# A two-layer decoder kernel: two more gate/up groups as seven products, with weight sums made earlier

## The chip, the cores and the metric

The kernel runs on one core of one Trainium2 chip. The metric is the device time of one execution in microseconds; lower is better. One execution was also recorded by the hardware profiler. In this text PE is TensorE (matmuls), DVE is VectorE, ACT is ScalarE, POOL is GpSimd and SP is the engine whose queue issues the DMA transfers. Each engine works through its own instruction queue in order; they meet by semaphores.

## The reference

Two decoder layers over 1024 tokens of width 1024, float32 throughout:

```python
for l in range(DEPTH):                       # 2
    h = rmsnorm(x, attn_norm[l])
    proj = h @ w_in[l]                       # one projection for four token mixers
    ...                                      # latent attention, gated convolution,
                                             # causal pooling, sliding-window attention
    x = x + mixed @ w_o[l]
    h2 = rmsnorm(x, ffn_norm[l])
    gate, up = jnp.split(h2 @ w_gate_up[l], 2, axis=-1)   # 1024 x 5632
    x = x + (jax.nn.silu(gate) * up) @ w_down[l]
return rmsnorm(x, final_norm)
```

The change concerns `h2 @ w_gate_up[l]` and what goes on around it.

## The kernel before

**Products.** A float32 product is made of three fp32r matmuls: both operands are split into a rounded high part and a low rest, and high·high, high·low and low·high are added in PSUM (`mm3`, L255). ACT makes the high part (a cast, L280, or a scaled copy with the norm's gain, L285) and DVE the low part (a subtraction, L283 or L286). A product of a 512 by 128 weight block with 512 by 512 activations is four such triples: 12 matmuls of 128x512.

**Gate/up in groups.** The 5632 columns of `w_gate_up` are worked in 22 groups `f`, each with 128 gate and 128 up columns. The 1024 inputs are taken as two halves and the 1024 tokens as two halves, so that a group is a 2 by 2 block product: eight products of 12 matmuls. From group 3 on a group is made by seven products (a Winograd form of Strassen's scheme), named after the activation operand: B11, B21, N2, N1, T3, B22, T4. They need four combined weight blocks and four combined activation blocks. B11, B21, B12 and B22 are the plain activation halves.

- `combine(j)` (L1117) makes the combined activations N1, N2, T3, T4 of block `j` (four blocks): two scaled copies on ACT, four operations on DVE, and four splits into high and low parts.
- `GateUp` (L1182) loads a group's two weight halves (two DMAs of 512 KB). `sums` (L1191) has POOL make three weight sums, `sum4` (L1215) the fourth; `split1` to `split4` split the weights and sums into high and low parts. `split_plain` splits the two raw halves only.
- Groups 0, 1 and 2 are plain: `plain(f, u)` (L1331) issues the four products of one token half `u`. `plain_gates` and `plain_acts` evacuate them: a multiplication with the row scale `r2` from the RMS norm, the silu on ACT, a scaling on POOL (L1370), and the product with the up half on DVE.

**Around it.** `out_last` (L1148) makes the last of the output projection, one token half at a time: eight outputs `d`, each an addition on DVE, a split with gain, a store to DRAM and a sum of squares for the norm. `ss2.rnorm` turns the sums into the row scale: a matmul against ones and three ACT operations (L349 to L351), two of which need a table other than the silu's. `combine` needs the outputs of both token halves. After it come groups 3 to 21 in a loop, whose weight sums are made two groups ahead.

**Memory.** `F` and `R` are pools of 128x512 float32 slots in SBUF for raw and split data (`half` takes one, `pair` two). A slot is waited for until its last reader is done. PSUM has eight banks of 128x512.

**What sets the order.** The program is traced in the order in which it is written and then planned: `Order` (L1715) estimates when each instruction could run on each engine (SP with eight transfers in flight), ranks them by what follows from them, picks the best of a few passes, assigns PSUM banks from the planned times, and imposes the order on each engine's queue. `need` (L1733 on) lists what each instruction has to wait for; `users` (L1747) adds waits for a slot's earlier users to the later users of a buffer.

Of the kernel before, what the change touches and what calls it, by code (L numbers as in the profile page):

```python
# [51 lines left out]
class Slots:  # L52
# [59 lines left out]
def trunk_kernel(ctx: ExitStack, tc: tile.TileContext, ins, out, given=None):  # L112
# [165 lines left out]
    def split(hi, lo, f, gain=None, after=None):  # L278
        if gain is None:
            a = act.copy(hi, f)  # L280
            if after is not None:
                behind(a, after)
            dve.tensor_tensor(out=lo, in0=f, in1=rd(hi), op=ALU.subtract)  # L283
        else:
            a = act.activation(hi, f, AF.Copy, scale=gain)  # L285
            dve.scalar_tensor_tensor(  # L286
                out=lo, in0=f, scalar=gain, in1=rd(hi), op0=ALU.mult, op1=ALU.subtract
            )
# [129 lines left out]
    for l in range(L):  # L418
# [698 lines left out]
        def combine(j):  # L1117

            (a0, b0), (a1, b1) = [[F.ap(x[2 * j + n][t]) for t in HALVES] for n in range(2)]
            c = PC_FFN + 2 * j  # L1120
            g0, g1, n = pcol(l, c), pcol(l, c + 1), l * NK + 2 * j + 1
            v0, v1 = tmp("te"), tmp("te")
            act.activation(v0, b0, AF.Copy, scale=g0)
            act.activation(v1, b1, AF.Copy, scale=g1)
            n1, n2, t3, t4 = tmp("tp"), tmp("tp"), tmp("tp"), tmp("tp")
            dve.scalar_tensor_tensor(
                out=n1, in0=a0, scalar=g0, in1=v0, op0=ALU.mult, op1=ALU.subtract
            )
# [13 lines left out]
            hb[T4][j] = half_split(t4)  # L1142
            for n in range(2):
                for u in range(2):
                    F.free(x[2 * j + n][u])
# [22 lines left out]
                for s in hl:  # L1168
                    R.free(s)

        def gu_load(f):
            raw = F.pair(), F.pair()
            for n in range(2):
                sp.dma_start(F.ap2(raw[n]), ins["w_gu"][l, f, n])
            return raw

        def pair_split(s, after=None):
            h, lo = R.pair(), R.pair()
            split(R.ap2(h), R.ap2(lo), F.ap2(s), after=after)
            return h, lo  # L1180

        class GateUp:  # L1182

            def __init__(self, f):
                self.raw = F.pair(), F.pair()
                for n in range(2):
# [14 lines left out]

            def split1(self):
                self.s1 = pair_split(self.raw[0])

            def split2(self):
                F.free_pair(self.raw[0])
                self.s2 = pair_split(self.raw[1])

            def split3(self):
                self.sq = pair_split(self.q)
                F.free_pair(self.q)

# [2 lines left out]
                pool.tensor_tensor(out=q4, in0=q4, in1=F.ap(self.raw[1] + 1), op=ALU.add)  # L1217

            def split4(self):
                self.s4 = half_split(F.ap(self.raw[1]))  # L1220
                F.free_pair(self.raw[1])

        def product(p, w, b, start=True, stop=True, again=False):
            terms = []
# [101 lines left out]
        std[1].split_plain()  # L1326


        acts = {f: [None, None] for f in range(3)}

        def plain(f, u):  # L1331

            w, b = std[f], ((B11, B21), (B12, B22))[u]
# [5 lines left out]
            waiting.append((f, u, pg, pu))  # L1339
            if u != (f == 2):  # L1340
                for i in w.s1 + w.s2:
                    R.free_pair(i)

# [3 lines left out]
        def plain_gates():  # L1347
            for f, u, pg, pu in waiting:
                gate = tmp("tp")
                mul_to(gate, pg, r2[u])  # L1350
                silu(gate, r2[u])
                gates.append((f, u, gate, pu))
            waiting.clear()

        def plain_acts():
            for f, u, gate, pu in gates:
                acts[f][u] = F.half()
                mul_to(F.ap(acts[f][u]), pu, gate)
            gates.clear()
# [139 lines left out]
        plain(0, 1)  # L1499
        std[2].split_plain()  # L1500
        combine(2)
        plain(1, 1)
        w = GateUp(3)
        plain_gates()
        w.sums()
        w.split1()
        combine(3)
        plain_acts()
        plain(2, 1)
# [6 lines left out]
        plain_acts()  # L1516
        wn = GateUp(4)
        plain(2, 0)
        w.sum4()
        w.split4()  # L1520
        wn.sums()
        plain_gates()
        plain_acts()
        sp.dma_start(ad_of(B11, 0), F.ap(acts[0][HALVES.index(0)]))
        combos(0)
        for f in range(3, NFF):
# [188 lines left out]
class Order:  # L1715
# [9 lines left out]
    def __init__(self, traced, edges, banks=True):  # L1725
        self.n = len(traced)
        self.engine = [self.queue(i) for i in traced]
        self.cost = [self.costs(i) for i in traced]
        self.kind = [self.kinds(i) for i in traced]
        self.moved = [self.passing(i) for i in traced]  # L1730
        place = {i.name: k for k, i in enumerate(traced)}
        need = [{} for _ in traced]
        users = self.users = defaultdict(list)  # L1733
        for k, i in enumerate(traced):
            for m in {a.memref for a in (*i.outs, *i.ins) if hasattr(a, "memref")}:
                users[m].append(k)
# [373 lines left out]
```

## Time and profile before

| | |
|---|---|
| median of 3 runs | 2056.87 us (2054.34 to 2056.95) |
| profiled execution, its own time | 2056.29 us |
| its span, first to last instruction | 2054.5 us |
| mean granted TensorE clock | 0.998 |
| PE, DVE, ACT, POOL busy | 2039.0, 1509.7, 984.6, 526.5 us |
| DMA traffic | 290.81 MB, mean 142 GB/s |

The page of the profile shows one execution. Its first part gives each engine's busy time, its share of the span and its instructions. The second part cuts the span into 40 equal slices and gives the busy share of each in tenths. The fourth follows the chain of work that ended last back from the last instruction. Groups of instructions read: line, engine, operation, outputs from inputs, shapes, count, then busy time and mean duration in ns, then the idle time before them with what ended it. A timeline row reads: start, duration, engine, line, operation, operands, count and, in brackets, the idle time of the engine before it and who ended that. Two rows of DVE overlap a little: the next starts before the last has drained, so back-to-back work is counted from start to start.

### The profile page before, as it was taken

How to read it: one execution, taken by the hardware profiler on the slowest of the kernel's cores; microseconds unless marked ns; L12 is line 12 of the kernel's file. 1: busy time of each engine (PE TensorE's matmuls, PEld its weight loads, DVE VectorE, ACT ScalarE, POOL GpSimd, SP SyncE). 2: the span in 40 equal slices, each digit the busy share in tenths (PEclk: the TensorE clock that was granted, in tenths of full speed). 3: DMA queues.
4: the chain of work that ended last, by engine and by line, in shares of the span. 5: the costliest groups of instructions: out<-in, count | busy, mean ns of one | idle time of the engine just before them, and what ended most of it. 6: DMA issues, size and time to landing. Idle time of an engine off the chain costs nothing.

```text
span 2054.5 us, 26467 instructions
## 1 busy us (share of the span) xinstructions
PE 2039.0 (99%) x9470; PEld 1685.7 (82%) x9470; DVE 1509.7 (73%) x2423; ACT 984.6 (48%) x1723; POOL 526.5 (26%) x404
## 2 busy tenths in 40 slices
PE   9999999999999999999999999999999999999998
PEld 7887888888888888888888878877888888888887
DVE  8779978976677668555657898889766766775555
ACT  7447746843333335444533666667333333354342
POOL 0000000046776772000000000000567767710000
PEclk9999999999999999999999999999999999999999
DMA  5101222425555547766401112133355555487642
GB/s 182 45 32 46 86 77 75 159 108 172 182 168 189 179 166 258 248 211 214 145 31 44 37 44 96 60 111 124 112 183 182 172 186 176 151 302 235 205 170 96
DMA packets 138083, 290.81 MB, mean 142 GB/s; under 512 B 13408, under 2 KB 60512, under 8 KB 137952
## 3 DMA queue, kind: packets, MB, share of 16 engines
q1 hardware_dynamic: 137952, 289.13, 41.2%
q8 instruction: 74, 1.21, 0.2%
q14 instruction: 57, 0.47, 0.1%
HBM read 204.66 MB, written 83.36 MB: 140 GB/s over the span
## 4 chain that ended last, share of the span: by engine, by line
PE 94%; DVE 3%; DMA 1%; ACT 1%; issue 1%; SPq 0%; DVEq 0%; POOL 0%; ACTq 0%
PE ps_mm L260 36%; PE ps_s L260 28%; PE ps_t L260 12%; PE ps_pv L260 8%; PE ps_pv L1025 2%; PE ps_t L1013 1%; PE ps_s L959 1%; PE ps_s L960 1%; PE ps_s L961 1%; PE ps_pv L634 1%; DMA u<-in_w_gu 1%; PE ps_s L573 1%; PE ps_s L831 1%; PE ps_t L622 1%; PE ps_t L343 1%
## 5 line engine op out<-in xcount | busy, mean ns | idle before, releaser
L260 PE MATMUL ps_mm<-u,u 128*128 128x512 f32 (+1 forms) x3376 | 829.1, 390 | 1.3 <-DVE u L1064 1.0
L260 PEld LDWEIGHTS ps_mm<-u,u 128*128 128x128 f32 x3376 | 614.7, 188 | 126.8 <-issue 4.6
L260 PE MATMUL ps_s<-u,u 128*128 128x512 f32 x2676 | 634.2, 389 | 1.3 <-DVE u L359 0.4
L260 PEld LDWEIGHTS ps_s<-u,u 128*128 128x128 f32 x2676 | 501.8, 188 | 108.5 <-DVE u L283 1.0
L283 DVE TENSOR_TENSOR u<-u,u 128x1024 fp32r<-128x1024 f32 (+2 forms) x392 | 457.8, 1184 | 158.9 <-ACT u L280 97.0
L280 ACT CAST u<-u 128x1024 fp32r<-128x1024 f32 (+2 forms) x392 | 339.1, 883 | 486.5 <-PE ps_mm L260 186.3
L260 PE MATMUL ps_t<-u,u 128*128 128x512 f32 (+1 forms) x1212 | 274.1, 378 | 0.3 <-DVE u L1363 0.3
L260 PEld LDWEIGHTS ps_t<-u,u 128*128 128x128 f32 x1212 | 219.0, 188 | 43.1 <-DVE u L1363 0.7
L1370 POOL TENSOR_TENSOR tp<-tp,u 128x512 f32<-128x512 f32 x88 | 145.3, 1651 | 348.9 <-ACT tp L1369 348.9
L1022 POOL MEMSET u<- 128x128 f32 x32 | 5.4, 205 | 880.6 <-PE ps_mm L260 418.2
L260 PE MATMUL ps_pv<-u,u 128*128 128x512 f32 x696 | 164.9, 389 | 0.0
L260 PEld LDWEIGHTS ps_pv<-u,u 128*128 128x128 f32 x696 | 130.6, 188 | 27.1
L1369 ACT ACTIVATE tp<-tp 128x512 f32<-128x512 f32 x88 | 55.6, 632 | 153.9 <-DVE tp L359 153.8
L280 ACT CAST u<-ps_t 128x512 fp32r<-128x512 f32 (+3 forms) x132 | 65.3, 503 | 51.3 <-PE ps_t L1013 25.9
L1448 POOL TENSOR_TENSOR u<-u 128x352 f32<-128x352 f32 x64 | 79.3, 1239 | 38.9 <-DMA u<-in_w_dn 34.0
L1217 POOL TENSOR_TENSOR u<-u 128x512 f32<-128x512 f32 x38 | 78.4, 2063 | 23.3 <-DVE u L283 22.1
L285 ACT ACTIVATE u<-u,par 128x512 fp32r<-128x512 f32 x100 | 69.9, 716 | 25.4 <-DVE u L359 7.9
L283 DVE TENSOR_TENSOR u<-ps_t,u 128x512 fp32r<-128x512 f32 (+3 forms) x132 | 75.5, 581 | 7.4 <-ACT u L280 6.5
L286 DVE SCALAR_TENSOR_TENSOR u<-u,par,u 128x512 fp32r<-128x512 f32 x100 | 73.2, 746 | 6.5 <-ACT u L285 6.4
L359 DVE TENSOR_TENSOR tp<-tp,u 128x512 f32<-128x512 f32 x76 | 75.6, 994 | 1.2
L1580 DVE TENSOR_TENSOR tp<-ps_mm,tn 128x512 f32<-128x512 f32 x38 | 26.3, 691 | 65.3 <-PE ps_mm L260 65.3
L324 ACT ACTIVATE tn<-u 128x512 f32<-128x512 f32 (+1 forms) x91 | 52.2, 596 | 44.2 <-DVE u L1633 41.0
(195 smaller groups left out, 2266.6 us busy)
## 6 DMA issues: line engine op xcount, KB each, us to landing
u<-in_w_gu SPq DMA_DIRECT2D x88, 512.0 KB, 3.8
ad<-u SPq DMA_DIRECT2D x154, 256.0 KB, 2.1
u<-ad SPq DMA_DIRECT2D x70, 512.0 KB, 5.2
u<-in_w_dn SPq DMA_DIRECT2D x64, 352.0 KB, 3.5
qd<-u SPq DMA_DIRECT2D x64, 352.0 KB, 2.6
u<-qd SPq DMA_DIRECT2D x32, 512.0 KB, 4.6
u<-in_w_in SPq DMA_DIRECT2D x28, 512.0 KB, 3.5
u<-in_w_dn SPq DMA_DIRECT2D x24, 512.0 KB, 4.9
```

The source lines that it names most:

```text
L260: pe.matmul(o, w, r, start=start and k == 0 and i == 0, stop=stop and k == n - 1 and i == 2, skip_group_check=again,)
L280: a = act.copy(hi, f)
L283: dve.tensor_tensor(out=lo, in0=f, in1=rd(hi), op=ALU.subtract)
L285: a = act.activation(hi, f, AF.Copy, scale=gain)
L286: dve.scalar_tensor_tensor(out=lo, in0=f, scalar=gain, in1=rd(hi), op0=ALU.mult, op1=ALU.subtract)
L324: act.activation(q, f, AF.Square)
L359: dve.tensor_tensor(out=o, in0=a, in1=b, op=ALU.mult)
L1025: pe.matmul(py[:, c0:], v_of(j, h), R.ap(s)[:, c0:], start=j == 0 and n == 0, stop=j == nj - 1 and n == 1,)
L1217: pool.tensor_tensor(out=q4, in0=q4, in1=F.ap(self.raw[1] + 1), op=ALU.add)
L1369: last_silu = act.activation(g, g, AF.Silu)
L1370: pool.tensor_tensor(out=g, in0=g, in1=r, op=ALU.mult)
L1448: pool.tensor_tensor(out=o, in0=a, in1=b, op=ALU.add)
```

## The change

Only group 0 stays plain. Groups 1 and 2 (`early`) are made by seven products too, both groups interleaved product by product by the new methods `start`, `n2`, `n1`, `t3`, `b22` and `t4`. Their weight sums don't come from `sums` and `sum4` in the gate/up part: a new function `premake` in the input projection loads the two weight halves (two DMAs of 512 KB a group), has POOL make the four sums, and stores the results in DRAM (two DMAs of 512 KB). The gate/up part loads from there: one sum as half of `raw[1]`, the pair `q` in `split3` (512 KB) and the last in `split4` (256 KB). In the planner, waits for a slot's earlier users are now taken from every instruction that writes the buffer, not from its first user alone, and given to all its users; the whole program is planned anew with it.

```diff
@@ input projection
+        def premake(f):
+
+            w1, w2, q = F.pair(), F.pair(), F.pair()
+            for n, i in enumerate((w1, w2)):
+                sp.dma_start(F.ap2(i), ins["w_gu"][l, f, n])
+            a11, a22, a12, a21 = F.ap(w1), F.ap(w1 + 1), F.ap(w2), F.ap(w2 + 1)
+            pool.tensor_tensor(out=F.ap(q + 1), in0=a21, in1=a22, op=ALU.add)
+            pool.tensor_tensor(out=F.ap(q), in0=a21, in1=a11, op=ALU.add)
+            pool.tensor_tensor(out=a21, in0=F.ap(q + 1), in1=a11, op=ALU.add)
+            pool.tensor_tensor(out=a12, in0=a12, in1=a21, op=ALU.add)
+            made = dpool.tile([P, 4 * HT], F32, name=f"gd{l}_{f}")
+            sp.dma_start(made[:, : 2 * HT], F.ap2(q))
+            sp.dma_start(made[:, 2 * HT :], F.ap2(w2))
+            for i in (w1, w2, q):
+                F.free_pair(i)
+            return made
+
+        prepared = {f: premake(f) for f in (1, 2)}
@@ class GateUp
-            def __init__(self, f):
+            def __init__(self, f, made=None):
+                self.f, self.made = f, made
                 self.raw = F.pair(), F.pair()
-                for n in range(2):
-                    sp.dma_start(F.ap2(self.raw[n]), ins["w_gu"][l, f, n])
+                sp.dma_start(F.ap2(self.raw[0]), ins["w_gu"][l, f, 0])
+                if made is None:
+                    sp.dma_start(F.ap2(self.raw[1]), ins["w_gu"][l, f, 1])
+                else:
+                    sp.dma_start(F.ap(self.raw[1]), ins["w_gu"][l, f, 1, :, :HT])
+                    sp.dma_start(F.ap(self.raw[1] + 1), made[f][:, 3 * HT :])
...
             def split3(self):
+                if self.made:
+                    self.q = F.pair()
+                    sp.dma_start(F.ap2(self.q), self.made[self.f][:, : 2 * HT])
                 self.sq = pair_split(self.q)
                 F.free_pair(self.q)
...
             def split4(self):
+                if self.made:
+                    s = F.half()
+                    sp.dma_start(F.ap(s), self.made[self.f][:, 2 * HT : 3 * HT])
+                    self.s4 = half_split(F.ap(s))
+                    F.free(s)
+                    return
                 self.s4 = half_split(F.ap(self.raw[1]))
                 F.free_pair(self.raw[1])
+
+            def start(self):
+                self.pa, pd = ps("aa"), ps("ad")
+                product(self.pa, blocks(self.s1, 0), hb[B11])
+                k1 = snap(self.pa)
+                product(pd, blocks(self.s2, 0), hb[B21])
+                self.own = [F.half()]
+                self.gate = F.ap(self.own[0])
+                dve.tensor_tensor(out=self.gate, in0=pd, in1=k1, op=ALU.add)
+                mul_to(self.gate, self.gate, r2[0])
+
+            def n2(self):
+                onto(self.pa, blocks(self.s2, 1), hb[N2])
+                for i in self.s2:
+                    R.free_pair(i)
+                self.own.append(F.half())
+                self.gate1 = F.ap(self.own[1])
+                act.copy(self.gate1, self.pa)
+                silu(self.gate, r2[0])
...
@@ order of the gate/up part
-        std = [GateUp(0), GateUp(1)]
-        std[0].split_plain()
+        std = GateUp(0)
+        std.split_plain()
+        early = [GateUp(f, prepared) for f in (1, 2)]
+        for w in early:
+            w.split1()
         out_last(HALVES[1], ma0)
...
-        plain(0, 0)
+        plain(0)
         r2.append(F.ap(ss2.rnorm(HALVES[0], tag="pv")))
+        plain_gates()
         combine(0)
-        plain(1, 0)
+        plain_acts()
+        for w in early:
+            w.split2()
+        early[0].start()
+        combine(1)
         r2.append(F.ap(ss2.rnorm(HALVES[1], tag="pv")))
-        plain_gates()
-        combine(1)
-        plain_acts()
-        std.append(GateUp(2))
-        plain(0, 1)
-        std[2].split_plain()
+        plain(1)
+        early[1].start()
         combine(2)
...
+        plain_acts()
+        combine(3)
+        for w in early:
+            w.n2()
+        for w in early:
+            w.split3()
+            w.n1()
+        for w in early:
+            w.t3()
+            w.split4()
+        w = GateUp(3)
+        for e in early:
+            e.b22()
+        w.sums()
+        w.split1()
         w.split2()
+        for e in early:
+            e.t4()
         w.split3()
-        plain_acts()
         wn = GateUp(4)
-        plain(2, 0)
         w.sum4()
         w.split4()
         wn.sums()
@@ planner, class Order
-        for ks in users.values():
-            for p in freed[ks[0]].difference(ks):
-                for k in ks[1:]:
+        for m, ks in users.items():
+            made = [freed[k] for k in ks if any(m == getattr(a, "memref", 0) for a in traced[k].outs)]
+            for p in set().union(*made).difference(ks):
+                for k in ks:
                     if p < ks[0]:
                         need[k][p] = True
```

More of the change, by code (lines that the diff above doesn't have):

```diff
@@ L1205, in split1 @@
                 self.s1 = pair_split(self.raw[0])
+                if self.made:
+                    F.free_pair(self.raw[0])
             def split2(self):
-                F.free_pair(self.raw[0])
+                if not self.made:
+                    F.free_pair(self.raw[0])
                 self.s2 = pair_split(self.raw[1])
+                if self.made:
+                    F.free_pair(self.raw[1])
             def split3(self):
+                if self.made:
+                    self.q = F.pair()
+                    sp.dma_start(F.ap2(self.q), self.made[self.f][:, : 2 * HT])
                 self.sq = pair_split(self.q)
@@ new lines, in n2, with n1 @@
+            def n2(self):
[6 more added lines that the diff above has]
+                silu(self.gate, r2[0])
+            def n1(self):
+                self.pc = ps("ac")
+                product(self.pc, blocks(self.sq, 1), hb[N1])
+                self.own.append(F.half())
+                self.up = F.ap(self.own[2])
+                act.copy(self.up, self.pc)
@@ new lines, in t3, with b22 @@
+            def t3(self):
+                onto(self.pa, blocks(self.sq, 0), hb[T3])
+                for i in self.sq:
+                    R.free_pair(i)
+                dve.tensor_tensor(out=self.up, in0=self.pa, in1=self.up, op=ALU.add)
+            def b22(self):
+                onto(self.pc, tuple(R.ap(i) for i in self.s4), hb[B22])
+                for i in self.s4:
+                    R.free(i)
+                dve.tensor_tensor(out=self.gate1, in0=self.pc, in1=self.gate1, op=ALU.add)
+                mul_to(self.gate1, self.gate1, r2[1])
@@ L1223, in product, with t4 @@
+            def t4(self):
+                onto(self.pa, blocks(self.s1, 1), hb[T4])
+                for i in self.s1:
+                    R.free_pair(i)
+                acts[self.f] = [F.half(), F.half()]
+                neg_mul(F.ap(acts[self.f][0]), self.pa, self.gate)
+                silu(self.gate1, r2[1])
+                neg_mul(F.ap(acts[self.f][1]), self.up, self.gate1)
+                for i in self.own:
+                    F.free(i)
         def product(p, w, b, start=True, stop=True, again=False):
@@ L1325, in trunk_kernel, with plain @@
                 R.free_pair(i)
-        std[1].split_plain()
         acts = {f: [None, None] for f in range(3)}
-        def plain(f, u):
-            w, b = std[f], ((B11, B21), (B12, B22))[u]
+        def plain(u):
+            w, b = std, ((B11, B21), (B12, B22))[u]
             pg, pu = ps("wide"), ps("wide")
@@ L1338, in plain @@
             product(pu, blocks(w.s1, 1), hb[b[1]], False, True)
-            waiting.append((f, u, pg, pu))
-            if u != (f == 2):
+            waiting.append((0, u, pg, pu))
+            if u:
                 for i in w.s1 + w.s2:
@@ L1488, in dn_start @@
                 cur.extend(dn_acts(order[0], (len(cur) + 1) // 2))
-        plain(0, 0)
+        plain(0)
         r2.append(F.ap(ss2.rnorm(HALVES[0], tag="pv")))
+        plain_gates()
         combine(0)
-        plain(1, 0)
-        r2.append(F.ap(ss2.rnorm(HALVES[1], tag="pv")))
-        plain_gates()
-        combine(1)
-        plain_acts()
-        std.append(GateUp(2))
-        plain(0, 1)
-        std[2].split_plain()
-        combine(2)
[L1502 to L1507, printed above, removed]
-        plain_acts()
-        plain(2, 1)
+        plain_acts()
[3 more added lines that the diff above has]
+        combine(1)
+        r2.append(F.ap(ss2.rnorm(HALVES[1], tag="pv")))
+        plain(1)
+        early[1].start()
+        combine(2)
         for hl in hb[B12]:
@@ L1521, in trunk_kernel @@
         wn.sums()
-        plain_gates()
-        plain_acts()
         sp.dma_start(ad_of(B11, 0), F.ap(acts[0][HALVES.index(0)]))
```

7 lines of the change are left out of this document (1 added, 6 removed).

## The prediction

> **What bounds the kernel now.** I read the busy shares and slices first, then the chain that ended last, then windows around the start of each layer's gate/up products, and last the vector and tensor timelines there.
>
> ```profile
> PE 2039.0 (99%) x9470; PEld 1685.7 (82%) x9470; DVE 1509.7 (73%) x2423; ACT 984.6 (48%) x1723; POOL 526.5 (26%) x404
> PE   9999999999999999999999999999999999999998
> DVE  8779978976677668555657898889766766775555
> PE 94%; DVE 3%; DMA 1%; ACT 1%; issue 1%; SPq 0%; DVEq 0%; POOL 0%; ACTq 0%
> 451.27 2.72 PE ps_s L260 x12
> 456.71 2.72 PE ps_s L260 x12
> ```
>
> TensorE (PE) works 2039.0 of 2054.5 us and is 94% of the chain. A product is 12 matmuls and takes 2.72 us, 0.2267 us each, with nothing between. A matmul less is therefore time less, unless PE then outruns its supply. Where would it? Where DVE is also full:
>
> ```profile
> 380.00:400.00 20.00, 20.00 (x89) 16.52 (x89) 20.00 (x33) 17.57 (x31) 0.00 (x0) 1.00 0.44 157
> 420.00:457.00 37.00, 37.00 (x164) 30.62 (x164) 28.39 (x37) 13.54 (x20) 17.46 (x11) 1.00 0.35 128
> 470.00:600.00 130.00, 130.00 (x575) 107.66 (x574) 88.71 (x89) 45.08 (x62) 90.21 (x66) 1.00 0.53 179
> 1410.00:1447.00 37.00, 37.00 (x162) 29.95 (x161) 33.99 (x50) 25.65 (x39) 6.87 (x5) 1.00 0.13 45
> ```
>
> The columns are the window, its length, then busy PE, weight load, DVE, ACT, POOL, the granted clock, the DMA share and GB/s. At 380 us PE and DVE are both at 100%; in layer 1 at 1410 DVE is at 92%. Here DVE makes the high/low halves of the activations and the four `combine` blocks. From 470 us on it is at 68% and has room. The clock is 1.00 throughout.
>
> **What is removed.** Groups 1 and 2 fall from 8 products to 7. That is 12 matmuls, two groups, two layers: 48 × 0.2267 = 10.88 us, 5.44 a layer. All of it is PE time on the path. It goes as long as PE is fed.
>
> **What it does to the supply.** Before, plain products of groups 1 and 2 need only the plain halves and can run while `combine` works. After, from the third product on, both groups need combined blocks. So I laid PE's and DVE's instruction orders in the changed program, which are fixed before anything runs, beside each other and timed DVE by its start-to-start distances in this trace:
>
> ```profile
> 402.84 0.75 DVE L286 SCALAR_TENSOR_TENSOR u<-u,par,u 128x512 fp32r<-128x512 f32 x1
> 404.10 2.73 DVE L286 SCALAR_TENSOR_TENSOR u<-u,par,u 128x512 fp32r<-128x512 f32 x4
> 425.11 1.21 DVE L283 TENSOR_TENSOR u<-u,u 128x1024 fp32r<-128x1024 f32 x1
> 426.24 0.68 DVE L283 TENSOR_TENSOR u<-tp,u 128x512 fp32r<-128x512 f32 x1
> 426.85 0.68 DVE L359 TENSOR_TENSOR tp<-ps_s,u 128x512 f32<-128x512 f32 x1
> 427.45 1.18 DVE L1126 SCALAR_TENSOR_TENSOR tp<-u,par,te 128x512 f32<-128x512 f32 x1
> ```
>
> That is 0.60 us for 128x512, 0.66 with a gain column ((2.73 − 0.75) / 3), 1.14 for 128x1024. One `combine` is 2 × 0.66 + 6 × 0.60 = 4.92, four are 19.7. From the first add of the last output half to the last piece that an N2 product needs, layer 0 has 65 × 0.60 + 25 × 0.66 + 3 × 1.14 = 58.9 us, 59.6 with its end. PE has 274 matmuls ahead of that product: 62.1 us. DVE is 2.5 us early by bare sums. The scale for the second token half and the second low half of a reloaded weight sum leave 1.7 and 2.0. The same in layer 1 gives 3.0, 2.2, 2.3 and 1.8. I take 2.0 and 1.8 as what DVE may be late. How late does it run against bare sums? These rows of before tell:
>
> ```profile
> 366.98 0.68 DVE L1162 TENSOR_TENSOR u<-u,ps_s 128x512 f32<-128x512 f32 x1
> 408.02 0.69 DVE L359 TENSOR_TENSOR u<-ps_s,tp 128x512 f32<-128x512 f32 x1 [1.18 <-POOL tp L1370]
> 439.24 0.68 DVE L359 TENSOR_TENSOR tp<-ps_s,u 128x512 f32<-128x512 f32 x1
> 1382.37 0.69 DVE L1162 TENSOR_TENSOR u<-u,ps_s 128x512 f32<-128x512 f32 x1 [0.62 <-PE ps_s L260]
> 1426.54 0.69 DVE L359 TENSOR_TENSOR u<-ps_s,tp 128x512 f32<-128x512 f32 x1 [1.92 <-POOL tp L1370]
> 1444.49 2.30 DVE L283 TENSOR_TENSOR u<-u,u 128x1024 fp32r<-128x1024 f32 x1
> 1446.72 0.68 DVE L359 TENSOR_TENSOR u<-ps_mm,tp 128x512 f32<-128x512 f32 x1
> 371.10 0.47 PE L260 MATMUL ps_s<-u,u 128*128 128x512 f32 x1 [0.31 <-DVE u L1162]
> 1378.51 0.50 PE L340 MATMUL ps_t<-u,ones_r 128*128 128x512 f32 x1 [1.23 <-ACT u L280]
> 1387.50 1.43 PE L260 MATMUL ps_s<-u,u 128*128 128x512 f32 x5 [0.36 <-DVE u L286]
> 1393.77 3.06 PE L260 MATMUL ps_mm<-u,u 128*128 128x512 f32 x12 [0.95 <-DVE u L1064]
> ```
>
> From 366.98 to 426.85 are 59.9 us against 56.4 of bare sum: 3.4 late. To 439.24 it is 72.3 against 64.8, 7.5 late, the rest coming beside group 3's weight sums on POOL (L1126 above took 1.18). In layer 1 from 1382.37 to 1446.72 it is 64.3 against 57.1: 7.2 late, 1.9 of it a wait for POOL's scaling (1426.54) and 1.2 beside a weight sum (2.30 for 1.14).
>
> Layer 0: 3.4, one more wait for a gate's scaling on POOL (1.2, as at 408.02) since the changed order has two of them before the N2 pieces end, less the 0.3 that PE itself lost there (371.10), less 2.0: PE waits 2.3 us, where it waited 0.3, so +2.0. Group 3's sums come later than this in the changed order and don't count. Layer 1: 7.2 − 1.2 − 1.3 (PE's own 0.36 and 0.95) − 1.8 = 2.9 in place of 1.3, so +1.6. The 1.23 at 1378.51 lies ahead and stays. Together **+3.6**. Bounds: no lateness and the old waits of 1.6 gone, −1.6; all the lateness of the rows against the same spare time, 5.5 + 5.4 − 1.6 = +9.3. I stand nearer the middle because the order of before, with less room early, showed only 1.6 of waiting.
>
> **Weight sums on POOL in the input projection.** Eight POOL sums a layer:
>
> ```profile
> L1195 POOL TENSOR_TENSOR u<-u,u 128x512 f32<-128x512 f32 x38 | 49.8, 1311 | 13.0 <-DVE u L283 11.0 <-PE ps_s L260 2.0
> L1196 POOL TENSOR_TENSOR u<-u,u 128x512 f32<-128x512 f32 x38 | 51.4, 1353 | 0.0
> L1197 POOL TENSOR_TENSOR u<-u,u 128x512 f32<-128x512 f32 x38 | 58.0, 1527 | 1.7
> L1217 POOL TENSOR_TENSOR u<-u 128x512 f32<-128x512 f32 x38 | 78.4, 2063 | 23.3 <-DVE u L283 22.1 <-DMA u<-in_w_dn 1.2
> L1379 DVE TENSOR_TENSOR u<-u,u 128x512 f32<-128x512 f32 x22 | 32.6, 1480 | 11.0 <-PE ps_t L260 8.6 <-DMA qd<-u 2.2
> L359 DVE TENSOR_TENSOR u<-u,u 128x512 f32<-128x512 f32 x38 | 24.6, 683 | 0.1
> 40.00:100.00 60.00, 60.00 (x311) 50.43 (x310) 47.64 (x126) 28.66 (x77) 0.00 (x0) 1.00 0.10 34
> 1040.00:1100.00 60.00, 60.00 (x301) 50.19 (x301) 37.15 (x98) 21.27 (x56) 0.00 (x0) 1.00 0.07 23
> ```
>
> One group is 1.31 + 1.35 + 1.53 + 2.06 = 6.25 us, two are 12.5, and POOL is idle there. What hurts is DVE: an add of two SBUF inputs takes 1480 ns where POOL sums run and 683 elsewhere. In 12.5 us DVE loses at most 12.5 × (1 − 683/1480) = 6.7 us, at least nothing. It is 79% busy in layer 0 and 62% in layer 1 and PE there waits for nothing, so I take **+0.5** for both layers.
>
> The Trainium skill's page "SBUF — State Buffer" (section "SBUF: two separate sides") goes further: POOL and a DVE operation with two SBUF inputs take a shared port in turn, each locking it for its whole instruction. By that DVE could stand for the whole 12.5 us. The trace agrees only in part: the loss is 0.80 us an operation, less than any of the four sums lasts; the rule is a rival below.
>
> Four loads and four stores of 512 KB join SP's queue; the DMA share there is 0.10 and 0.07. The stores wait for POOL, and behind the first stands a slice of the input weights. PE issues 61 matmuls (13.8 us) between that slice's place and its use; no cost. The memsets behind the sums on POOL come far later.
>
> **Reloads.** Per layer the two sums q (512 KB) and two quarters (256 KB) come back:
>
> ```profile
> u<-ad SPq DMA_DIRECT2D x70, 512.0 KB, 5.2
> 358.41 8.29 DMA u<-in_w_gu
> ```
>
> Group 1's q goes into a buffer that `combine(2)` still reads; its cast heads ACT's in-order queue, with the scalings for `combine(3)` and a gate's silu behind it. From that read's end (47.5) to `combine(3)`'s first DVE operation (54.7) are 7.2 us; cast and scaling take 1.6, which leaves 5.6 for a transfer whose like has a median of 5.2. Nothing is added, but the cover is thin. The extra work of the seven-product form, ten operations a layer on DVE (under 7 us) and on ACT, falls behind the tight stretch, where DVE is at 68%.
>
> **Sum.** Against the profiled execution, 2056.29 us (span 2054.5): 2056.29 − 10.88 + 3.6 + 0.5 = 2049.5. The median of the runs stands 0.6 above that execution: **2050.1**.
>
> **The rivals.**
> - *DVE keeps up.* No waits there: 2056.9 − 10.9 − 1.6 = 2044.4, up to 2046. For it: bare sums leave 1.7 to 3.0 us everywhere. Against: before had more such waits with plain work at hand.
> - *DVE becomes the bound.* Upper lateness: 2056.9 − 10.9 + 9.3 + 0.5 = 2055.8. For it 100% at 380 us; against it, part of that lateness came beside sums that now run later.
> - *POOL locks DVE out in the projection.* DVE stands 12.5 us a layer, makes up its idle share (21% and 38%), and half its operations are hit (an estimate): (9.9 + 7.7) / 2 = 8.8, so 2058.4. Against: 0.80 us a hit.
> - *The q reload comes late.* Group 2's reload stands directly before group 1's in SP's order. If one takes 8.29 and the other 5.2 behind it, group 1's lands after 13.5, not 5.6: 7.9 a layer held on ACT, then `combine(3)`, then PE, 15.8 in all, 2065.9: **slower**. It decides from about 3.4 a layer, a landing after 9.0. For it the 8.29 row; against it, few transfers run at that time (DMA share 0.13 and 0.35 in the last windows above).
> - *The new order costs elsewhere.* Every engine's order is planned afresh from the added dependences. PE idles 15.5 us in all now; a third more is 5, so 2055.
>
> **How the numbers follow.** Forecast 0.59, DVE keeps up 0.10, DVE the bound 0.11, POOL lock 0.05, late reload 0.12, order elsewhere 0.03. What a measurement of this kernel tells from no change is 0.2%, 4.1 us. Faster: 0.56 of the forecast and 0.10; slower: the reload and 0.01 of the lock; the rest within. The likeliest case alone reaches from 2047 to 2053. The range, 2044.6 to 2058.0, takes in both ends of the DVE cost and leaves out the late reload and the tails.
>
> **What would show it.** Right: 48 matmuls fewer, PE busy down by about 10.9, PE waits of 2 to 4 us a layer before N2 pieces, ended by DVE, and none over 1 us in the input projection. Wrong: PE waiting there for DVE splits beside POOL sums; ACT waiting on the `gd` reload before its cast; or PE idle growing away from both places.

## The result, and the profile after

The changed kernel takes **2063.24 us** (median of 6 runs, 2062.66 to 2067.84); the kernel before, run beside it, 2055.53 (6 runs, 2054.34 to 2056.95). The ratio is 1.0041, 95% interval 1.0028 to 1.0054: slower by some 8 us, where 2050.1 was forecast. The profiled executions have spans of 2061.2 and 2054.5 us.

From the page of the changed kernel: busy times, slices of PE and DVE, the chain that ended last by engine.

```profile
PE 2035.3 (99%) x9422; PEld 1673.6 (81%) x9422; DVE 1503.7 (73%) x2443; ACT 992.6 (48%) x1743; POOL 577.3 (28%) x420
PE   9999999999999999999999999999999999999998
DVE  8779979987666667655657898889866655585555
PE 68%; POOL 7%; DVE 5%; DMA 4%; issue 2%; ACT 2%; SPq 0%; DVEq 0%; POOLq 0%; ACTq 0%
```

The 48 matmuls are gone (9470 to 9422 records), yet PE's busy time fell by 3.7 us, not 10.9, and the span grew by 6.7. PE's share of the chain fell from 94% to 68% while POOL's rose from nothing to 7%. PE is now fed late, and POOL is in the path. The slices of PE still read 9 throughout: at a loss of 1% they show nothing.

To find the place I summed, over all matmuls of a stretch of the span, the time to the next matmul's start above the fastest tenth of its line and shape ("PE time lost", us; worked out from the two traces):

```
stretch of the span    before   after
0-360    projection      35.2    37.3   layer 0
360-480  transition       1.1     7.4
480-820  gate/up loop     1.6     4.9
820-1040                  0.7     0.7
1040-1360 projection     30.4    29.3   layer 1
1360-1480 transition      6.4     4.9
1480-1840 gate/up loop    1.3     9.5
1840-end                  3.5     3.5
sum                      80.2    97.5
```

The saving of 10.9 against 17.3 more lost gives +6.4, and the spans differ by 6.7. "Transition" is where the prediction put all the waits. **Most of the loss is elsewhere: +11.5 in the two loops, of groups 3 to 21, whose code the change does not touch.** Windows of the loops say it without any sum of mine; the columns are as in the prediction, before first:

```profile
470.00:800.00 330.00, 329.68 (x1455) 272.59 (x1454) 228.55 (x227) 115.00 (x158) 226.12 (x164) 1.00 0.52 176
1480.00:1810.00 330.00, 330.00 (x1457) 273.27 (x1456) 226.14 (x225) 112.95 (x156) 233.34 (x167) 1.00 0.52 176
```

and after:

```profile
470.00:800.00 330.00, 327.83 (x1437) 269.16 (x1438) 212.30 (x227) 113.00 (x157) 241.16 (x165) 1.00 0.53 177
1480.00:1810.00 330.00, 326.50 (x1420) 264.82 (x1419) 210.94 (x224) 108.44 (x152) 244.56 (x167) 1.00 0.52 173
```

Read the counts of matmuls: in the same 330 us PE starts 18 fewer in layer 0 and 37 fewer in layer 1, times 0.2267 us 4.1 and 8.4 us. Busy PE shows only 1.9 and 3.5 of it, since ends of matmuls are modelled. POOL is busy 15.0 and 11.2 us longer with one instruction more and with as many, DVE 16.3 and 15.2 us less with one or two fewer.

The timeline of the changed kernel's PE in layer 1's loop, and the same stretch on POOL, ACT and DVE:

```profile
1697.23 2.88 PE L260 MATMUL ps_pv<-u,u 128*128 128x512 f32 x12
1699.95 2.88 PE L260 MATMUL ps_s<-u,u 128*128 128x512 f32 x12
1703.06 3.03 PE L260 MATMUL ps_t<-u,u 128*128 128x512 f32 x12 [0.23 <-DVE u L1447]
1706.06 3.02 PE L260 MATMUL ps_s<-u,u 128*128 128x512 f32 x12
1708.92 2.88 PE L260 MATMUL ps_mm<-u,u 128*128 128x512 f32 x12
1711.64 2.88 PE L260 MATMUL ps_s<-u,u 128*128 128x512 f32 x12
```

```profile
1692.92 2.27 POOL L1243 TENSOR_TENSOR u<-u 128x512 f32<-128x512 f32 x1
1697.42 1.29 POOL L1213 TENSOR_TENSOR u<-u,u 128x512 f32<-128x512 f32 x1
1698.67 1.39 POOL L1532 TENSOR_TENSOR u<-u,u 128x352 f32<-128x352 f32 x1
1700.09 1.05 ACT L280 CAST u<-u 128x1024 fp32r<-128x1024 f32 x1 [4.24 <-POOL u L1532]
1701.17 1.23 DVE L283 TENSOR_TENSOR u<-u,u 128x1024 fp32r<-128x1024 f32 x1 [1.92 <-ACT u L280]
1702.32 0.68 DVE L1447 SCALAR_TENSOR_TENSOR u<-ps_pv,tp 128x512 f32<-128x512 f32 x1
```

Read it from PE's wait backwards. The product at 1703.06 waits for DVE's operation at 1702.32, which reads the last of the product that held its PSUM bank before (the name `ps_t` doesn't tell the bank; the planner gives it); that stands in DVE's order behind a split, which waited 1.92 us for ACT's cast, which waited 4.24 us for a sum on POOL that ended at 1700.06. Nothing here is short of time on average; four in-order queues hand on one lateness. The bracket shows 0.23 us, but from product to product it is 3.11, 3.00 and 2.86 us instead of 2.72, 0.81 us in all. The like comes at 1586, 1664, 1742 and 1782 too, in most turns of the loop.

### The profile page after: what moved, and what is told of

It is laid out like the page before. It is cut to its first block, busy times and chain, and to the rows that moved or that the text cites. A ratio compares the mean times of both kernels' runs of the same rounds, so it can differ in the third digit from the quotient of the medians.

```text
span 2061.2 us, 26597 instructions
## 1 busy us (share of the span) xinstructions
PE 2035.3 (99%) x9422; PEld 1673.6 (81%) x9422; DVE 1503.7 (73%) x2443; ACT 992.6 (48%) x1743; POOL 577.3 (28%) x420
## 4 chain that ended last, share of the span: by engine, by line
PE 68%; POOL 7%; DVE 5%; DMA 4%; issue 2%; ACT 2%; SPq 0%; DVEq 0%; POOLq 0%; ACTq 0%
PE ps_mm L260 25%; PE ps_s L260 21%; PE ps_t L260 8%; PE ps_pv L260 6%; POOL u L1532 3%; PE ps_pv L1044 2%; PE ps_t L1032 1%; DMA u<-in_w_dn 1%; POOL tp L1454 1%; DMA ad<-u 1%; POOL u L1214 1%; DVE u L283 1%; POOL u L1213 1%; ACT u L280 1%; DMA u<-in_w_gu 1%
## 5 line engine op out<-in xcount | busy, mean ns | idle before, releaser
L283 DVE TENSOR_TENSOR u<-u,u 128x1024 fp32r<-128x1024 f32 (+2 forms) x400 | 443.3, 1126 | 225.2 <-ACT u L280 173.4
L280 ACT CAST u<-u 128x1024 fp32r<-128x1024 f32 (+2 forms) x400 | 345.1, 881 | 505.4 <-POOL u L1215 60.1
L260 PE MATMUL ps_t<-u,u 128*128 128x512 f32 (+1 forms) x1124 | 255.3, 378 | 2.8 <-DVE u L1447 2.7
L260 PEld LDWEIGHTS ps_t<-u,u 128*128 128x128 f32 x1124 | 201.6, 188 | 45.8 <-DVE u L1447 6.5
L1454 POOL TENSOR_TENSOR tp<-tp,u 128x512 f32<-128x512 f32 x80 | 135.1, 1689 | 341.7 <-ACT tp L1453 341.7
L260 PE MATMUL ps_pv<-u,u 128*128 128x512 f32 x744 | 177.8, 390 | 1.6 <-DVE te L1658 1.0
L260 PEld LDWEIGHTS ps_pv<-u,u 128*128 128x128 f32 x744 | 139.3, 188 | 32.1 <-ACT tn L1321 1.9
L1453 ACT ACTIVATE tp<-tp 128x512 f32<-128x512 f32 x80 | 50.5, 631 | 155.2 <-DVE tp L359 155.1
L749 POOL TENSOR_TENSOR u<-u,u 128x512 f32<-128x512 f32 x4 | 6.0, 1509 | 380.4 <-PE ps_t L622 288.9
L1532 POOL TENSOR_TENSOR u<-u 128x352 f32<-128x352 f32 x64 | 80.5, 1259 | 31.6 <-DMA u<-in_w_dn 30.2
L1532 POOL TENSOR_TENSOR u<-u,u 128x352 f32<-128x352 f32 x64 | 85.0, 1328 | 3.0
```

Source lines behind the costliest of these rows:

```text
L260: pe.matmul(o, w, r, start=start and k == 0 and i == 0, stop=stop and k == n - 1 and i == 2, skip_group_check=again,)
L1453: last_silu = act.activation(g, g, AF.Silu)
L1454: pool.tensor_tensor(out=g, in0=g, in1=r, op=ALU.mult)
L1532: pool.tensor_tensor(out=o, in0=a, in1=b, op=ALU.add)
```

## The experiments

What a run "loses" below is the PE time lost of the table above. Three theories stood for the loop. *POOL*: its sums last longer than the planner has them (1.31 us for 512 columns), and the new plan leaves them no margin. *Banks*: the planner gives each product the PSUM bank that was freed last, so that any lateness becomes a wait. *Planner hunk*: the change's new rule of waits for slots orders the loop worse. For the first transition: a chain of DVE and ACT that is late, or the banks.

**Banks exchanged (e1, e2).** The kernel before and the changed one, each with its instruction order kept on every engine; only PSUM banks are exchanged: in order of the trace, from a tile on, two banks change places where the planned rest between the last reader and the next product grows (up to 4 us).

```diff
-            best = found[0], banks, found[1]
+            best = found[0], plan.rest(banks, found[2]), found[1]
```

The function `rest`, which makes the exchanges, is left out here.

> The changed kernel with every engine's instruction order as it is; only the PSUM banks of some tiles are exchanged, so that a tile gets a bank whose last reader was done longer ago by the plan. Bank theory (a product stands at its first matmul because the planner gave it the bank that was freed last, with no time to spare): the waits behind L1447, L1658 and L1321 in the loop of groups 3 to 21 and the 2.3 us at 419 us go, 11 to 14 us in all, so 2049 to 2053 us. POOL theory (the sums on POOL hold up the chain and the bank only shows it): the waits move to the next product, 2060 us or more.

> The kernel before with the same exchange of banks and its own order. Bank theory: in its trace bank waits are under 2 us in all, so 2053 to 2056 us. POOL theory: no change, 2055 to 2056 us. A gain as large as in the changed kernel would say that the exchange helps for a reason of its own.

The changed kernel comes to 2057.65 us (1.0013, 1.0004 to 1.0022 of before), between the two expectations; the kernel before to 2052.58 (0.9988, 0.9978 to 0.9997), a little below both of its own. By the ratios the banks were worth 0.28% in the changed kernel, 5.8 us, and 0.12% in the old one, 2.5 us. With them e1 loses no more than before in the first projection (34.7), so the changed kernel's +2.1 there is the banks' too. But the loops of e1 still lose 3.2 and 7.4 us, and a wait in the transition has only moved:

```profile
425.35 3.83 PE L260 MATMUL ps_mm<-u,u 128*128 128x512 f32 x10 [2.71 <-ACT u L280]
1687.03 3.02 PE L260 MATMUL ps_pv<-u,u 128*128 128x512 f32 x12 [1.15 <-ACT tn L1321]
```

Where the bank no longer holds PE, ACT does. So the banks are a part of the loss, and of the rest they decide only who is named.

**The planner hunk alone, and with the weight sums (e3, e4).** e3 is the kernel before with the last hunk of the change; e4 adds to it the loads, POOL sums and stores of the input projection, and nothing reads them.

```diff
-        for ks in users.values():
-            for p in freed[ks[0]].difference(ks):
-                for k in ks[1:]:
+        for m, ks in users.items():
+            made = [freed[k] for k in ks if any(m == getattr(a, "memref", 0) for a in traced[k].outs)]
+            for p in set().union(*made).difference(ks):
+                for k in ks:
                     if p < ks[0]:
```

```diff
+        def premake(f):
...
+        prepared = {f: premake(f) for f in (1, 2)}
```

> The kernel before with the change's rule for waits in the planner alone. Planner theory (that rule makes the loop of groups 3 to 21 slower): 8 to 12 us more, 2063 to 2068 us. Bank theory: only what the newly drawn banks happen to give, 2053 to 2059 us, with the loop's period at 38.1 us for two groups if no bank is drawn tight.

> The kernel before with the changed planner and the weight sums made and stored in the input projection, but not used: groups 1 and 2 stay plain. Projection theory (POOL sums beside DVE, eight more transfers): 2 us or more over the planner alone in the first 360 us and from 1035 to 1370 us. Bank theory: within 1.5 us of the planner alone there; what is more comes from bank waits in the loop.

e3 takes 2061.57 us (1.0026, 1.0014 to 1.0037), between its two expectations and in neither: the hunk alone costs some 5 us by the ratio, but not where it was looked for. Its loops lose 2.6 and 3.0, 2.7 more than before in all; its first transition loses 6.8, 5.7 more, most of it by one wait at the norm of the second token half and slow matmuls behind it (last section). From e3's timeline:

```profile
415.42 8.06 PE L260 MATMUL ps_mm<-u,u 128*128 128x512 f32 x27 [2.01 <-DVE tn L352]
```

e4 takes 2061.37 (1.0025, 1.0014 to 1.0035). **The sums in the projection cost next to nothing**: −0.2 us against e3, less than either interval, and in the projections' PE time lost e4 stands 0.1 above e3 in each layer.

**The planner hunk with exchanged banks (e7).** e3 with the edit of e1.

> The kernel before with the changed planner rule, in its own order, and banks exchanged as in the first two runs. Bank theory: the 2.0 us behind L352 at 415 us and the slower matmuls after it (1.6 us) go, 2056 to 2058 us. Supply theory (DVE and ACT are late there whatever the bank): the wait moves to the next product, 2060 to 2062 us.

2054.91 us (0.9995, 0.9986 to 1.0005): a little below both expectations. The wait at 415 is gone, the first transition loses 3.5, and the loops lose 1.8 and 2.4. With three plain groups, then, the bank was the cause of e3's wait. The new rule by itself explains little of the loop's loss: 2.7 us with the banks of e3 and 1.3 with these, of 11.5.

**POOL's other work in the loop made short (e8).** The changed kernel, same order and banks; the sums for the down product (L1532) work on 16 of 352 columns when it runs, and are planned at their full size. This leaves out most of these sums, so only the time is of use.

```diff
+            k = 16 if THIN else CW
...
-                pool.tensor_tensor(out=o, in0=a, in1=b, op=ALU.add)
+                pool.tensor_tensor(out=o[:, :k], in0=a[:, :k], in1=b[:, :k], op=ALU.add)
```

> The changed kernel, every engine's order and the banks as they are; the 128 sums of down weights on POOL work on 16 of 352 columns, which leaves out most of that work on POOL. POOL theory: with POOL early, the casts of weight sums on ACT and with them DVE come in time and the loop's waits, 11.5 us more than before, go: 2052 to 2055 us. Bank theory: the waits behind L1447 stay, as the banks are the same: 2060 us or more.

2052.63 us (0.9979, 0.9969 to 0.9988). From e8's windows:

```profile
470.00:800.00 330.00, 329.04 (x1452) 272.10 (x1451) 215.18 (x229) 116.52 (x158) 175.77 (x167) 1.00 0.53 178
1480.00:1810.00 330.00, 329.04 (x1452) 272.13 (x1451) 215.05 (x229) 116.94 (x158) 176.66 (x168) 1.00 0.53 178
```

POOL is relieved of some 65 us a window and PE makes 1452 matmuls, 15 and 32 more, in the same order and with the same banks; the loops lose 1.0 and 2.3. DVE is not what was relieved: it takes 0.94 us an instruction in these windows, as in the changed kernel. The loop's loss is POOL's lateness. The first transition is not helped: it loses 9.5, here with slow matmuls behind its wait (last section).

**Less DVE work ahead of the transition (e10).** The changed kernel, same order and banks; the additions of the sums of squares work on 16 columns (`THIN` is set when it runs), and are planned at their full size.

```diff
-                dve.tensor_tensor(out=a, in0=a, in1=q, op=ALU.add)
+                k = 16 if THIN and self.n == D else cols.stop - cols.start
+                dve.tensor_tensor(out=a[:, :k], in0=a[:, :k], in1=q[:, :k], op=ALU.add)
```

> The changed kernel, orders and banks as they are; DVE adds the squares for the norms on 16 of 512 columns, which leaves out some 6 us of DVE a layer ahead of the combined activations. Supply theory (DVE comes late to the combined blocks): the waits at 419, 429 and 1444 us shrink by 3 to 5 us in all, 2058 to 2060 us. Order theory (ACT's table loads, silu and casts in its queue set those waits): less than 1.5 us of change, 2062 to 2064 us.

2061.06 us (1.0022, 1.0012 to 1.0031), between the two expectations. The first transition loses 6.0 instead of 7.4, its longest wait 1.44 instead of 2.34. Part of it is DVE's time, part stays; the run doesn't tell the theories apart.

**The planner told what POOL takes (e11, e12, e15).** Nothing computed changes: a POOL sum of 512 columns is planned as 1.6 us (e11 and e12) or 1.8 (e15, with 0.0035 in the line below) instead of 1.3, and the program is planned anew. e11 and e15 have the exchanged banks of e1, e12 has not.

```diff
-                return 0.03 + n * 0.0025, n * 0.0025 - 0.01
+                return 0.03 + n * 0.0031, n * 0.0031 - 0.01
```

These are the rows of the changed kernel's groups that the number comes from:

```profile
L1213 POOL TENSOR_TENSOR u<-u,u 128x512 f32<-128x512 f32 x38 | 54.5, 1435 | 8.2 <-PE ps_s L260 4.5 <-DMA u<-in_w_gu 3.7
L1214 POOL TENSOR_TENSOR u<-u,u 128x512 f32<-128x512 f32 x38 | 60.2, 1584 | 0.0
L1215 POOL TENSOR_TENSOR u<-u,u 128x512 f32<-128x512 f32 x38 | 59.1, 1555 | 0.8
L1532 POOL TENSOR_TENSOR u<-u,u 128x352 f32<-128x352 f32 x64 | 85.0, 1328 | 3.0
```

1435 to 1584 ns against 1310 planned, and 1328 against 910 for 352 columns. Undisturbed they take about 1.28 and 0.95 us in this trace; what is above that is time in which DVE holds POOL up (last section).

> The changed kernel with exchanged banks, planned anew with a POOL sum of 512 columns estimated at 1.6 us (as long as they take in its trace) in place of 1.3. POOL theory: the plan leaves room behind POOL's sums, the loop's period for two groups returns to 38.1 us: 2050 to 2056 us. If POOL's length is not what the loop lacks: as with exchanged banks alone, 2056 to 2060 us.

> The changed kernel planned with a POOL sum at 1.6 us in place of 1.3, with the banks as the plan gives them (no exchange). POOL theory: the loop's waits are gone as with both (2048.6 us), and only bank waits are left, 2049 to 2053 us. If the exchange of banks did the work there: 2055 us or more.

> The changed kernel with exchanged banks and a POOL sum estimated at 1.8 us. POOL theory: any estimate that covers the 1.6 us measured keeps the loop free of waits: 2046 to 2051 us. If 1.6 hit a lucky order: 2054 us or more.

e11: 2048.62 us (0.9961, 0.9947 to 0.9976). e12: 2050.39 (0.9976, 0.9966 to 0.9986). e15: 2047.24 (0.9960, 0.9945 to 0.9975). e12 differs from the changed kernel in this one estimate and is 0.65% better; its loops lose 1.0 and 1.1, its transitions no less (8.6 and 6.5). From e11's windows:

```profile
470.00:800.00 330.00, 330.00 (x1457) 273.25 (x1456) 230.62 (x230) 117.04 (x160) 231.23 (x165) 1.00 0.56 179
```

All 1457 matmuls are there, with every POOL sum at its full size. In the changed kernel it was the plan's margin, not POOL's capacity.

**The same estimate for three plain groups (e13).** e7 with the edit of e11.

> The kernel before with the changed planner rule, POOL at 1.6 us and exchanged banks: the same planner as the run at 2048.6 us, without the change to groups 1 and 2. POOL theory: its loop waits were 1.6 and 1.3 us to begin with, so little is to be had, 2052 to 2056 us, and the change itself is worth 4 to 8 us with an equal planner. Rival: the planner's estimate helps any kernel as much, 2047 to 2050 us, and the change is worth nothing.

2058.64 us (1.0012, 1.0002 to 1.0021), outside both expectations: it got worse than e7, and its loops lose 4.4 and 4.8. So the estimate isn't better as such. Beside e11, which has the same planner, estimate and exchange of banks, the change is worth 0.0051 of 2055.7, 10.5 us. That this is about its 10.9 of matmuls is luck: e13 loses 7.1 us more than e11 in the loops, and e11 loses 6.8 more than e13 in the transitions (8.4 and 5.4 against 2.9 and 4.1). Beside e2, the fastest version with three plain groups that was run, it is worth 0.0027 or 5.5 us.

**The evacuation of group 0 later (e14).** e11 with the gates and silus of group 0's first token half written behind the second norm, so that ACT no longer changes between the norm's tables and the silu's and back.

```diff
-        plain_gates()
         combine(0)
-        plain_acts()
...
         r2.append(F.ap(ss2.rnorm(HALVES[1], tag="pv")))
+        plain_gates()
+        plain_acts()
```

> The run at 2048.6 us with the gates of group 0 (silu and all) written behind the second norm, so that ACT loads tables once in this stretch of a layer and not four times. Table theory: the waits of 6 us more than before between 360 and 480 us are the 3 x 1.28 us of loads in ACT's queue a layer, so 2 to 4 us less in the first layer and 1 to 3 in the second: 2042 to 2046 us. Supply theory (DVE's own work is what comes late): within 1.5 us, 2047 to 2050 us.

2044.66 us (0.9948, 0.9933 to 0.9963): **the fastest version, 11 us under the kernel before.** The transitions lose 5.0 and 4.0, where e11's lose 8.4 and 5.4. In the changed kernel's groups stand these table loads,

```profile
L1453 ACT ACT_TABLE_LOAD x4 | 5.1, 1283 | 0.1
L349 ACT ACT_TABLE_LOAD x2 | 2.6, 1283 | 0.9 <-PE ps_pv L340 0.9
L350 ACT ACT_TABLE_LOAD x2 | 2.6, 1283 | 0.0
```

and in e14's only this one of them (three loads at other lines are the same in both):

```profile
L1453 ACT ACT_TABLE_LOAD x2 | 2.6, 1283 | 0.9 <-DVE tp L359 0.7
```

Six fewer, three a layer, 3.8 us of ACT a layer at its busiest. The gain over e11 is 0.13%, 2.7 us by the ratios, which is less than half the width of either interval. The program is planned anew here too, so how much of it is the loads and how much the new order was not told apart.

## Why the prediction was wrong

**The matmuls: right.** 48 fewer, 10.9 us. e11 fits the sum: its span is 8.5 us under that of before, the 10.9 saved less some 2.4 more lost.

**The tight stretch: right place, wrong share.** Forecast +2.0 and +1.6. Measured +6.3 in layer 0 (5.2 without the loop's first wait, at 470) and −1.5 in layer 1, +4.8 in all; that the two together come near the forecast is luck. In layer 1 the old waits of 1.23, 0.36 and 0.95 us are gone, of which the prediction had kept the first, and one of 1.53 has come. In layer 0 the longest wait is one that the prediction didn't have: ahead of the N2 products, at the second norm. From the changed kernel's timeline of PE, ACT and DVE:

```profile
419.35 3.04 PE L260 MATMUL ps_s<-u,u 128*128 128x512 f32 x12 [2.34 <-DVE tn L352]
429.68 2.56 PE L260 MATMUL ps_mm<-u,u 128*128 128x512 f32 x10 [0.73 <-ACT u L280]
470.26 3.03 PE L260 MATMUL ps_pv<-u,u 128*128 128x512 f32 x12 [0.96 <-DVE te L1658]
1444.08 2.56 PE L260 MATMUL ps_mm<-u,u 128*128 128x512 f32 x10 [1.53 <-ACT u L280]
411.27 1.28 ACT L349 ACT_TABLE_LOAD   x1
413.69 1.28 ACT L350 ACT_TABLE_LOAD   x1
417.17 0.61 ACT L351 ACTIVATE tn<-tn 128x512 f32<-128x512 f32 x1
413.70 0.69 DVE L283 TENSOR_TENSOR u<-tp,u 128x512 fp32r<-128x512 f32 x1 [0.58 <-ACT u L280]
416.67 0.69 DVE L283 TENSOR_TENSOR u<-tp,u 128x512 fp32r<-128x512 f32 x1 [1.14 <-ACT u L280]
418.61 0.68 DVE L352 SCALAR_TENSOR_TENSOR tn<-ps_pv,tn 128x512 f32<-128x512 f32 x1
```

The norm's three ACT operations, with two table loads and four other operations among them, take from 411.27 to 417.78, and DVE's operation behind them ends at 419.29. The prediction summed DVE alone; but DVE stood idle 0.58 and 1.14 us here for ACT's casts, and it worked without a pause from 416.67 on. By these rows ACT's queue, with the table loads in it, was the longer one up to there; no run takes it out alone.

**The sums in the projection: smaller than forecast.** +0.5 was taken; e4 shows 0.1 a layer. From the windows of the changed kernel at the sums:

```profile
80.00:130.00 50.00, 49.12 (x241) 40.59 (x240) 38.38 (x88) 19.64 (x49) 10.97 (x8) 1.00 0.35 119
97.04 0.62 PE L634 MATMUL ps_pv<-u,u 128*128 128x256 f32 x3 [0.83 <-DVE u L283]
```

In 50 us with eight POOL instructions PE idles 0.88 us, nearly all of it in one wait. e1, with the same sums in the same order, doesn't lose even that against before. The rival in which POOL locks DVE out falls as a cost, not as a mechanism: DVE is locked out (last section), but at these sums its operations take 3.1 and 3.2 us a layer longer in all, where the rival had it stand for the whole 12.5, and next to none of it reaches PE. The prediction's argument against the lock, that an operation lost 0.80 us and so less than a whole sum, does not hold: one that comes while a sum is under way waits only for the rest of it.

**The q reload: the rival falls.** From the changed kernel's timeline, the two loads of q in layer 0, the second one's cast and what stands before it on ACT, the like in layer 1, and the one cast of the whole profile that waits for a reload, that of a last sum:

```profile
413.63 5.41 SPq L1237 DMA_DIRECT2D u<-gd  x2
426.77 1.28 ACT L1453 ACT_TABLE_LOAD   x1
428.60 1.03 ACT L280 CAST u<-u 128x1024 fp32r<-128x1024 f32 x1
1442.99 1.03 ACT L280 CAST u<-u 128x1024 fp32r<-128x1024 f32 x1
437.03 0.62 ACT L280 CAST u<-u 128x512 fp32r<-128x512 f32 x1 [0.24 <-DMA u<-gd]
```

No cast of q waits for its transfer, in either layer; the rival had 7.9 us a layer. But PE's waits at 429.68 and 1444.08 end with these casts (429.63 and 1444.02), and each stood directly behind a table load and a silu on ACT. The cast did come late, through ACT's own queue.

**The step that failed** is the sentence that the extra work "falls behind the tight stretch, where DVE is at 68%". It costed the loop at nothing from the busy share of one engine. Measured, the loops lose 11.5 us more than before; "PE idle growing away from both places" was one of the prediction's own signs of being wrong. What decided was whether POOL's sums come in time in an order planned anew, where their casts follow closely: e8 (shorter sums, same plan) and e12 (same sums, another plan) each remove the loss. One reason for POOL's lateness can be counted: of the 114 sums of L1213 to L1215 54 began during a DVE operation that held them up, and beyond 1.28 us each they took 27.9 us in all; before (L1195 to L1197) it was 26 of 114 and 13.3 us. The warning stood in a row that the prediction quotes for another purpose: POOL's sums at 1311, 1353, 1527 and 2063 ns, against the 1310 that the planner takes for each. The old plan held with the same low figure; e13 loses time in the loops with three plain groups and the better one. So it was not the early groups' work that filled the loop, but one plan with less margin than another.

**The rival "the new order costs elsewhere" was the true one.** Its mechanism was right and its size off: priced at 5 us with a chance of 0.03, it measured 11.5 in the loops, 12.6 with the wait at 470. e12 takes the loops' 11.5 away with one number in the plan.

**What stays open.** How much of layer 0's +6.3 is ACT's loads, DVE's work and the banks; why the plan of e13 waits more with the better estimate; what the table loads alone are worth in e14; and why a wait of 0.23 us costs PE 0.81 in three products (the timeline at 1703).

## What to carry to other kernels

When a program is planned anew, a local change can be paid for where its code doesn't reach: compare counts of matmuls in equal windows of the untouched loops first, since busy shares hide it. A planner's durations are better tried at those of the loaded engine, here POOL beside DVE, because in-order queues turn a lateness of 0.2 us an operation into waits of PE: that took the loss away in the changed kernel (e12) and is no guarantee (e13). Where only the plan is at fault, changing one estimate tells it before any code is rewritten.

## What the runs showed of the hardware

**DVE and POOL hold each other up for whole instructions.** In 470 to 800 us DVE and POOL together are busy 454.7 us before and 453.5 after (the rows above); but with the new order POOL's part rose by 15.0 and DVE's fell by 16.3. Rows of the changed kernel's loop show how; the third stands above too:

```profile
1691.16 1.80 POOL L1454 TENSOR_TENSOR tp<-tp,u 128x512 f32<-128x512 f32 x1 [7.12 <-ACT tp L1453]
1692.54 1.51 DVE L283 TENSOR_TENSOR u<-u,u 128x1024 fp32r<-128x1024 f32 x1 [0.73 <-ACT u L280]
1692.92 2.27 POOL L1243 TENSOR_TENSOR u<-u 128x512 f32<-128x512 f32 x1
```

POOL's first operation ends at 1692.96. DVE's, which came during it, ends 1.09 us later, and POOL's second, which came during DVE's, 1.14 us after that. Counted over the changed kernel's trace: 180 DVE operations (TENSOR_TENSOR) with two inputs in SBUF began during a POOL operation, and 166 of them ended 0.55 us (512 columns) or 1.08 us (1024) after it, within 0.03; 87 of 512 columns with one input in PSUM took 0.68 to 0.69 us all the same. In turn, 142 POOL operations of 512 columns began during a DVE operation with two inputs in SBUF, and 136 of them ended 1.15 us after it; the other 114 took 1.3 us each. The Trainium skill's page "SBUF — State Buffer" (section "Who interferes with whom") says that issue order decides which of the two is blocked. The trace agrees: whichever comes second waits for the other's end.

**A short wait of PE can halve its clock.** Of the seven waits of 2.0 to 2.8 us in all profiles, five were followed by seven to nine matmuls at about twice the usual distance, up to 0.43 us. In e12 two waits of 0.90 and 1.39 us, the second 2.6 us after the first, did it too (granted clock 0.67 from 410 to 415 us). From e1's windows, behind the wait that ended at 425.35:

```profile
425.00:430.00 5.00, 4.65 (x13) 3.72 (x14) 3.82 (x8) 1.95 (x4) 1.26 (x1) 0.66 0.42 157
```

and from those of the changed kernel, behind its 2.34 us:

```profile
420.00:425.00 5.00, 5.00 (x24) 4.10 (x23) 4.94 (x9) 2.58 (x5) 0.00 (x0) 1.00 0.26 98
```

The granted clock is 0.66 in the one and 1.00 in the other; e1's ten matmuls took 3.83 us, where the like took 2.56 at 429.68 in the changed kernel. The Trainium skill's page "TensorE: Matmul & The Clock Gate" (section "What's actually happening") has the throttle watch free-running windows of about 3.4 us. That e3's wait of 2.0 us was enough and this one of 2.34 was not agrees with windows that run free. The same page of the Trainium skill (section "HAM oscillation — how this bites in real kernels") puts the limit at idle gaps of more than about 3.4 us; these runs do not bear that out.
